# More up products ahead of the down products: 47 instead of 39, six of them behind the last one-hot product

## The chip, the cores and the metric

The kernel runs on one core of one Trainium2 chip. The metric is the time of one execution in device microseconds (us). The kernel before took 1903.67 us, the median of three runs (1903.01 to 1905.06).

Engines are named as the profile names them: PE is TensorE (PEld its weight loads), DVE VectorE, ACT ScalarE, POOL GpSimd, SP SyncE. SP issues the ordinary transfers of this kernel, in order, and POOL issues the indexed gathers.

## The reference, cut to what matters

The block is attention plus a gated recurrence (untouched here), and then PEER, a lookup of 128 single-neuron experts (8 heads, 16 each) out of 16384 for each of 512 tokens:

```python
def one_block(hb):                       # 128 tokens of h = RMSNorm(x)
    ...                                  # sc: scores of 8 heads x 2 x 128 keys
    top_s, pos = lax.top_k(cand_s, PEER_TOPK)
    idx = jnp.take_along_axis(cand_i, pos, axis=-1)      # i1 * 128 + i2
    g = jax.nn.softmax(top_s, axis=-1)
    u = u_tab[idx]
    act = jax.nn.gelu(jnp.einsum('thkd,td->thk', u, hb))
    wts = (g * act.astype(jnp.float32)).astype(hb.dtype)
    v = v_tab[idx]
    return jnp.einsum('thk,thkd->td', wts, v)
...
x = x + peer_ffn(rms_norm(x, norm2_g), w_peer_q, peer_sub_keys, peer_u, peer_v)
```

## The kernel before, in words

The 512 tokens are four blocks of 128. Two blocks gather the rows of `u` and `v` of their own experts (`experts()`): for each of 128 experts per token POOL issues one gather of 128 rows of 8 KB (tile `uv`, 1.05 MB), DVE multiplies the u half with the token and sums (L862), ACT makes the weight (L867, L868), and DVE adds the weighted v half to the result (L845). The second of these blocks (`second()`, tiles `h2g`, `x1g`) runs beside the part that follows; `share()` doles out its experts: 0.2 for each up product of `ups_far`, 0.5 for each one-hot group, 0.6 for each down product alone, and 1.1 for each down product with an up product beside it. A gather is placed behind the last gelu, copy or `o` product then written (`turn[0]`).

The other two blocks (256 tokens) are done densely over all 16384 experts, in 128 chunks of 128. Three kinds of products make this up:

- **Up products** (`up()`, 128): one chunk of `u` (512 KB) against the 256 tokens, then gelu into a tile `y`. The first 39 in the order of `TURN` are *ahead* (`c < AHEAD`): `u` as it is, in fp32, against `p1.h2r`, 8 matmuls which the trace shows as 16. The other 89 are *near*: `chunk()` splits `u` into a high and a low fp32r part (an ACT cast, L906, and a DVE subtraction, L907), and three products of parts are summed, 24 matmuls against `p1.h2T`, the operand that the keys used too.
- **One-hot products** (`wbuild()`, 16 groups of 16 tokens): DVE writes one-hot tiles `o2` (L994), DVE, POOL and ACT write weighted one-hot tiles `o1s`, PE multiplies them into `pw`, ACT copies to `wst`, and SP stores each group to DRAM (`w_d`, 1 MB). A load turns `w_d` into `w`, the weight of every expert of a chunk for all 256 tokens; it comes in tiles of 12 chunks (1.5 MB), the first in three pieces, the last of which (L1023, groups 14 and 15) needs the last group's store.
- **Down products** (`down()`, 128): DVE makes `o = y * w` (L1035), and PE adds `o` times the chunk of `v` into `acc`, 8 matmuls of 128x512. One load brings two chunks of `v` (1 MB, L1031).

The order in the program: 26 up products ahead (`LEAD`, `ups_far`, psum tile `pup`) stand beside the last picks of the keys on DVE (L258 to L334). `picks_t` turns the picks on PE (tile `pt`). Then come the 16 one-hot groups, with one up product (psum tile `st`) after each while fewer than `AHEAD - 6` are made, and a loop for the rest. Then come 128 down products; from down product 24 on (`HEAD`) each one has a near up product behind it, until all 128 are made. Results ahead wait in 24 slots of two `rg` tiles and 15 tiles of the pool `mid`. Everything carries an order from a scheduler at build time: an up product written behind the last one-hot group may be put ahead of it where its operands allow.

The pool `ap` (the keys' operand `p1.h2T`, two parts of 128x2048) is open to the end of the kernel. `trunk` holds pools of the earlier part, and its room is given to `mid` when it closes.

## Time and profile before

| | us |
|---|---|
| median of 3 runs | 1903.67 |
| the profiled execution | 1902.58 |
| its span in the profile | 1900.8 |
| PE busy | 1742.3 (92%) |
| DVE busy | 1309.5 (69%) |
| ACT busy | 781.8 (41%) |
| PE, down products (`acc`) | 449.9, 1024 matmuls |
| PE, near up products (`st<-a,t`) | 282.2, 2136 matmuls |
| PE, up products ahead (`pup`, `st<-r,u`) | 90.6 and 48.1, 416 and 208 matmuls |

Busy time is time in which an engine had an instruction of its own running. The chain that ended last goes from the last instruction backward, at each step to what released it; idle time of an engine counts only where the chain goes through what it waited for. The part that the change touches lies from 1015 us to the end: the last picks (to 1046), one-hot products beside up products (to 1116), one-hot products alone (to 1175), a junction (to 1194), 24 down products alone (to 1277), down and near up products in turn (to 1845), and 16 last down products. Matmul records can be missing by a few per cent.

### The profile page before, as it was taken

The numbers are of one execution on the slowest core, as the hardware profiler recorded it, in microseconds if no ns is written. First come the engines' busy times: TensorE is split into PE (matmuls) and PEld (weight loads), VectorE is DVE, ScalarE is ACT, GpSimd is POOL, SyncE is SP. The second block draws the span as 40 slices with busy tenths as digits, with TensorE's granted clock in tenths as the row PEclk, the third lists the DMA queues.
The fourth block names the chain that finished last, engine by engine and source line by source line (L and its number), as shares of the span: only waits on it lengthen the run. The fifth ranks groups of instructions, "written<-read, shape, count | busy, mean of one in ns | idle before, by whom it ended". The sixth has DMA issues, their size and how long they took to land.

```text
span 1900.8 us, 25745 instructions
## 1 busy us (share of the span) xinstructions
PE 1742.3 (92%) x9166; PEld 1371.8 (72%) x9166; DVE 1309.5 (69%) x2818; ACT 781.8 (41%) x2193; POOL 483.3 (25%) x375
## 2 busy tenths in 40 slices
PE   7899898889959899979996984899999999999998
PEld 6689797778849677769985884346776677667763
DVE  2241387989999987689999467446676667666662
ACT  3382333767768744254412565012322232222210
POOL 1100001535332233242001365222222232222220
PEclk9899897889969899999998998899999999999999
DMA  7478554887888899987464578999999999999893
GB/s 297 144 272 315 181 186 158 308 291 269 328 287 298 322 400 356 369 310 255 153 220 144 183 274 310 356 373 393 370 367 389 378 365 369 348 350 363 328 354 122
DMA packets 131471, 563.37 MB, mean 296 GB/s; under 512 B 11408, under 2 KB 43280, under 8 KB 88592
## 3 DMA queue, kind: packets, MB, share of 16 engines
q1 hardware_dynamic: 94480, 293.29, 42.6%
q0 software_dynamic: 36864, 268.45, 37.3%
q8 instruction: 72, 1.18, 0.2%
q14 instruction: 55, 0.45, 0.1%
HBM read 539.68 MB, written 22.02 MB: 296 GB/s over the span
## 4 chain that ended last, share of the span: by engine, by line
PE 60%; DVE 14%; issue 9%; DMA 8%; ACT 5%; POOL 3%; DVEq 0%; SPq 0%; POOLq 0%; ACTq 0%
PE acc L210 22%; PE st L210 16%; DMA uv<-in_uv_dram,idx 6%; PE ppq L210 5%; PE pkq L210 5%; POOL uv L855 3%; DVE x1f L845 2%; DVE uv L862 2%; PE pw L1010 1%; PE pvv L210 1%; DMA v<-in_v_t_dram 1%; PE pgt L210 1%; PE psc L511 1%; DVE wl L231 1%; PE pbR L687 1%
## 5 line engine op out<-in xcount | busy, mean ns | idle before, releaser
L855 POOL DMA_INDIRECT uv<-in_uv_dram,idx x256 | 360.0, 1406 | 1067.6 <-DVE x1g L845 265.7
L210 PE MATMUL acc<-v,o 128*128 128x512 f32 x1024 | 449.9, 595 | 20.8 <-DVE o L1035 18.6
L210 PEld LDWEIGHTS acc<-v,o 128*128 128x128 f32 x1024 | 191.8, 191 | 244.9 <-issue 222.4
L210 PE MATMUL st<-a,t 128*128 128x256 f32 x2136 | 282.2, 292 | 0.0
L210 PEld LDWEIGHTS st<-a,t 128*128 128x128 f32 x2136 | 262.5, 191 | 22.5 <-issue 19.6
L845 DVE SCALAR_TENSOR_TENSOR x1g<-uv,e,x1g 128x1024 f32<-128x1024 f32 x128 | 164.1, 1282 | 47.6 <-ACT e L868 47.6
L845 DVE SCALAR_TENSOR_TENSOR x1f<-uv,e,x1f 128x1024 f32<-128x1024 f32 x128 | 163.8, 1280 | 17.2 <-ACT e L877 17.0
L862 DVE SCALAR_TENSOR_TENSOR uv<-uv,h2f 128x1024 f32<-128x1024 f32 x128 | 155.6, 1218 | 28.9 <-DMA uv<-in_uv_dram,idx 28.5
L862 DVE SCALAR_TENSOR_TENSOR uv<-uv,h2g 128x1024 f32<-128x1024 f32 x128 | 155.9, 1218 | 19.6 <-DMA uv<-in_uv_dram,idx 19.6
L867 ACT ACTIVATE e<-e 128x1 f32<-128x1 f32 x128 | 25.9, 202 | 341.4 <-DVE uv L862 341.0
L907 DVE TENSOR_TENSOR t<-raw,t 128x1024 fp32r<-128x1024 f32 x89 | 108.8, 1223 | 74.5 <-ACT t L906 74.5
L1035 DVE TENSOR_TENSOR o<-y,w 128x256 f32<-128x256 f32 x104 | 44.0, 423 | 99.8 <-PE acc L210 99.7
L924 ACT ACTIVATE y<-st 128x256 f32<-128x256 f32 x89 | 34.1, 383 | 179.7 <-PE st L210 177.5
L231 DVE TENSOR_TENSOR wl<-raw,wh 128x1024 fp32r<-128x1024 f32 x76 | 90.9, 1217 | 23.8 <-PE pgt L210 9.5
L906 ACT CAST t<-raw 128x1024 fp32r<-128x1024 f32 x89 | 92.0, 1034 | 25.1 <-PE acc L210 25.1
L210 PE MATMUL pup<-r,u 128*128 128x256 f32 x416 | 90.6, 379 | 1.0 <-DMA u<-in_u_t_dram 1.0
L230 ACT CAST wh<-raw 128x1024 fp32r<-128x1024 f32 x76 | 76.7, 1043 | 28.2 <-PE pwo L714 10.4
L210 PEld LDWEIGHTS pup<-r,u 128*128 128x128 f32 x416 | 78.7, 190 | 12.3 <-issue 1.7
L1010 PE MATMUL pw<-o1s,o 128*128 128x128 f32 x512 | 68.8, 289 | 17.7 <-DVE o L994 13.3
L1009 POOL TENSOR_SCALAR o1s<-iota,r 128x128 f32<-128x128 bf16 x64 | 70.8, 1114 | 41.7 <-issue 14.8
L1010 PEld LDWEIGHTS pw<-o1s,o 128*128 128x128 f32 x512 | 64.5, 199 | 22.8 <-ACT wst L1011 5.7
L210 PE MATMUL pkq<-wh,a 128*128 128x256 f32 x384 | 77.8, 297 | 0.0
(266 smaller groups left out, 3235.5 us busy)
## 6 DMA issues: line engine op xcount, KB each, us to landing
v<-in_v_t_dram SPq DMA_DIRECT2D x64, 1024.0 KB
raw<-in_u_t_dram SPq DMA_DIRECT2D x89, 512.0 KB
u<-in_u_t_dram SPq DMA_DIRECT2D x39, 512.0 KB
w<-in_w_br_dram SPq DMA_DIRECT2D x16, 1024.0 KB
w_d<-wst SPq DMA_DIRECT2D x16, 1024.0 KB
w<-w_d SPq DMA_DIRECT2D x9, 1536.0 KB
w<-in_w_qkv_dram SPq DMA_DIRECT2D x12, 1024.0 KB
raw<-in_w_qkv_dram SPq DMA_DIRECT2D x24, 512.0 KB
```

The costliest lines, as they stand in the source:

```text
L210: nc.tensor.matmul(o, lhs[a], rhs[b], start=start and i == 0, stop=stop and i == len(terms) - 1)
L230: A.copy(hi[:, i : i + 1024], raw)
L231: V.tensor_tensor(lo[:, i : i + 1024], raw, hi[:, i : i + 1024].bitcast(F32), op=ALU.subtract)
L845: V.scalar_tensor_tensor(x1, v_, e_, x1, op0=ALU.mult, op1=ALU.add)
L855: i = nc.gpsimd.indirect_dma_start(out=t, out_offset=None, in_=uv, in_offset=bass.IndirectOffsetOnAxis(ap=idx[:, s : s + 1], axis=0),)
L862: i = V.scalar_tensor_tensor(t[:, 0:D], t[:, 0:D], 1.0, h2, op0=ALU.mult, op1=ALU.mult, accum_out=d)
L906: A.copy(t[:, 0, :], raw)
L907: V.tensor_tensor(t[:, 1, :], raw, t[:, 0, :].bitcast(F32), op=ALU.subtract)
L924: return A.activation(o, S_, AF.Gelu_apprx_tanh)
L1009: e.tensor_scalar(o1, iota, k1, g1, op0=ALU.is_equal, op1=ALU.mult)
L1010: nc.tensor.matmul(pw[:, j, :], o2[:, j, :], o1, start=True, stop=True)
L1035: turn[0] = V.tensor_mul(o.rearrange("p (g t) -> p g t", g=NG), yv, ws[c // WI][:, :, c % WI, :])
```

## The change

Eight more up products are ahead: 47. They come from eight results kept in a new tile `spare` (128 x 8 x 256).

- The pool `ap` becomes one of `trunk`'s, and the keys of the last three blocks are written ahead of `trunk.close()`. `mid` then lies where `p1.h2T` was as well. So the near up products take another operand: `h2s`, two tiles in `mid`, written by one ACT cast of `p1.h2r` and one DVE subtraction, both 128x2048 and both new instructions.
- `LEAD` goes from 26 to 31: five more up products stand in `ups_far`.
- The loop over the one-hot groups takes up products while fewer than `AHEAD - HELD` = 41 are made: 10 of them, where it was 7 (33).
- The last `HELD` = 6 are tied: the first matmul of each has an order dependence on the last one-hot product. It is one of the build order alone; at run time they are on the same engine. The 6 that were written behind the loop before had no tie.
- Near up products are 81 where they were 89, and the first is written behind down product 32 where it was 24. The shares of `second()` go with that.

```diff
-    HEAD, MID = 24, 15
-    AHEAD = HEAD + MID
+    HEAD, MID, SPARE = 24, 15, 8
+    AHEAD = HEAD + MID + SPARE
...
-    LEAD = 26
+    LEAD, HELD = 31, 6
...
-    def up(c, S_):
+    def up(c, S_, after=None):
         ks = lambda k: slice(k * P, (k + 1) * P)
         if c < AHEAD:
             u = wp.tile([P, D], F32, tag="raw", name=nm("u"), bufs=3)
             nc.sync.dma_start(u, u_t[c])
             for k in range(KT):
-                mm(S_, [u[:, ks(k)]], [p1.h2r[:, k, :]], k == 0, k == KT - 1)
+                i = mm(S_, [u[:, ks(k)]], [p1.h2r[:, k, :]], k == 0, k == KT - 1)
+                if after is not None and k == 0:
+                    tc.add_manual_dep(i.ins, after.ins.name, in_turn, reason="in turn")
         else:
             uhi, ulo = chunk(u_t, c, "near")
             for k in range(KT):
-                mm(S_, [uhi[:, ks(k)], ulo[:, ks(k)]], [h[:, k, P : 3 * P] for h in p1.h2T], k == 0, k == KT - 1)
+                mm(S_, [uhi[:, ks(k)], ulo[:, ks(k)]], [h[:, k, :] for h in h2s], k == 0, k == KT - 1)
...
         for tg in range(NG):
-            wbuild(tg)
+            last = wbuild(tg)
             share("w")
-            if len(ys) < AHEAD - 6:
+            if len(ys) < AHEAD - HELD:
                 up_near()
...
         wload(0, 14, NG)
         while len(ys) < AHEAD:
-            up_near()
+            up_near(last)
+
+        A.copy(h2s[0], p1.h2r)
+        V.tensor_tensor(h2s[1], p1.h2r, h2s[0].bitcast(F32), op=ALU.subtract)
         for c in range(NCH):
             down(c, ys[c])
-            if c >= HEAD and len(ys) < NCH:
+
+            more = c >= HEAD + SPARE and len(ys) < NCH
+            if more:
                 up_near()
-            share("both" if c >= HEAD and len(ys) < NCH else "down")
+            share("both" if more else "down")
```

The scheduler puts the two new instructions for `h2s` far ahead of where they are written: among the picks on DVE, near 936 us of the trace of before.

PE at the start of the one-hot stage, before (`pup` and `st` are up products, `pt3` turns the picks, `pw` are one-hot products):

```order
L210 MATMUL pup_1836_9261<-r_1193_6202,u_1837_9262 128x256 x8
L932 MATMUL pt3_1842_9286<-ident_92,r_1211_6281 128x128 x3
L932 MATMUL pt3_1843_9295<-ident_92,r_1211_6281 128x128 x3
L1010 MATMUL pw_1846_9318<-o1s_1844_9316,o2_1847_9319 128x128 x4
L1010 MATMUL pw_1849_9332<-o1s_1844_9316,o2_1850_9333 128x128 x4
L210 MATMUL st_1858_9375<-r_1193_6202,u_1859_9376 128x256 x7
L1010 MATMUL pw_1852_9346<-o1s_1844_9316,o2_1853_9347 128x128 x4
```

The same place after:

```order
L210 MATMUL pup_1848_9332<-r_1193_6202,u_1849_9333 128x256 x8
L938 MATMUL pt3_1854_9357<-ident_92,r_1211_6276 128x128 x3
L938 MATMUL pt3_1855_9366<-ident_92,r_1211_6276 128x128 x3
L210 MATMUL st_1870_9446<-r_1193_6202,u_1871_9447 128x256 x8
L210 MATMUL st_1888_9524<-r_1193_6202,u_1889_9525 128x256 x4
L1018 MATMUL pw_1858_9389<-o1s_1856_9387,o2_1859_9390 128x128 x4
L1018 MATMUL pw_1861_9403<-o1s_1856_9387,o2_1862_9404 128x128 x4
L210 MATMUL st_1888_9524<-r_1193_6202,u_1889_9525 128x256 x4
```

One and a half up products now stand between `pt3` and the first `pw`. Further on, before, 13 up products alternate with the one-hot products of the first 6 groups, and 10 groups follow alone; after, 10 up products alternate with the first 4 groups, and 12 groups follow alone.

PE at the junction, the end of the one-hot products and the first down products, before:

```order
L1010 MATMUL pw_2092_10368<-o1s_2084_10338,o2_2093_10369 128x128 x4
L1010 MATMUL pw_2095_10382<-o1s_2084_10338,o2_2096_10383 128x128 x4
L210 MATMUL acc_9315<-v_2113_10479,o_2114_10481 128x512 x4
L210 MATMUL acc_9315<-v_2113_10479,o_2115_10487 128x512 x4
L210 MATMUL acc_9315<-v_2118_10500,o_2119_10502 128x512 x4
```

And after:

```order
L1018 MATMUL pw_2110_10475<-o1s_2102_10445,o2_2111_10476 128x128 x4
L1018 MATMUL pw_2113_10489<-o1s_2102_10445,o2_2114_10490 128x128 x4
L210 MATMUL st_2118_10512<-r_1193_6202,u_2119_10513 128x256 x8
L210 MATMUL st_2120_10524<-r_1193_6202,u_2121_10525 128x256 x8
L210 MATMUL st_2122_10536<-r_1193_6202,u_2123_10537 128x256 x8
L210 MATMUL st_2124_10548<-r_1193_6202,u_2125_10549 128x256 x8
L210 MATMUL st_2126_10560<-r_1193_6202,u_2127_10561 128x256 x8
L210 MATMUL acc_9386<-v_2131_10588,o_2132_10590 128x512 x3
L210 MATMUL st_2128_10572<-r_1193_6202,u_2129_10573 128x256 x8
L210 MATMUL acc_9386<-v_2131_10588,o_2132_10590 128x512
```

Five of the six tied up products stand between the last one-hot product and the first down product, and the sixth inside the first down product.

SP at the same place, before (`w_d` are the last two groups' stores, `w` the loads of the weights, `v` those of the down products):

```order
L1012 DMA w_d_172<-wst_2071_10280 128x2048
L1031 DMA v_2113_10479<-in_v_t_dram 128x2x1024
L1031 DMA v_2118_10500<-in_v_t_dram 128x2x1024
L1031 DMA v_2123_10521<-in_v_t_dram 128x2x1024
L1012 DMA w_d_172<-wst_2085_10339 128x2048
L1023 DMA w_1979_9901<-w_d_172 128x2x192
L1023 DMA w_2112_10477<-w_d_172 128x16x192
```

And after:

```order
L1020 DMA w_d_172<-wst_2089_10387 128x2048
L1040 DMA v_2131_10588<-in_v_t_dram 128x2x1024
L1040 DMA v_2136_10609<-in_v_t_dram 128x2x1024
L1020 DMA w_d_172<-wst_2103_10446 128x2048
L1040 DMA v_2141_10630<-in_v_t_dram 128x2x1024
L919 DMA u_2125_10549<-in_u_t_dram 128x1024
L919 DMA u_2127_10561<-in_u_t_dram 128x1024
L1032 DMA w_1993_9984<-w_d_172 128x2x192
L919 DMA u_2129_10573<-in_u_t_dram 128x1024
L1032 DMA w_2130_10586<-w_d_172 128x16x192
```

The loads for the fourth to sixth tied up product now stand around the last piece of the first `w`, behind three loads of `v`. There are three buffers for `u`, so the fourth waits until the first tied up product has been computed.

## Rows read from the trace of the kernel before

**Rows 1.** The chain that ended last, 1040 to 1350 us: start, length, what
```profile
1042.79 1.23 DVE r L321
...
1110.53 1.80 PE pw L1010 x16
1112.35 0.70 DVE o L994
1113.21 8.70 DMA uv<-in_uv_dram,idx
...
1131.99 10.76 DMA uv<-in_uv_dram,idx
...
1176.36 14.34 DMA w_d<-wst
1190.72 2.65 DMA w<-w_d
1193.97 37.26 PE acc L210 x81
1231.23 22.39 DMA v<-in_v_t_dram
1253.76 24.27 PE acc L210 x56
...
1331.90 5.75 PE st L210 x48
1337.65 6.87 PE acc L210 x16
```

**Rows 2.** Timeline of PE: start, length, instructions, idle time before and its releaser
```profile
1015.65 10.60 PE L210 MATMUL pup<-r,u 128*128 128x256 f32 x48 [0.95 <-DMA u<-in_u_t_dram]
1037.93 0.88 PE L932 MATMUL pt<-ident,r 128*128 128x128 f32 x3 [11.68 <-DVE r L321]
1044.07 0.90 PE L932 MATMUL pt<-ident,r 128*128 128x128 f32 x3 [5.26 <-DVE r L321]
1046.43 3.78 PE L1010 MATMUL pw<-o1s,o 128*128 128x128 f32 x16 [1.46 <-ACT kTb L937]
...
1104.69 1.95 PE L1010 MATMUL pw<-o1s,o 128*128 128x128 f32 x16
1106.48 4.05 PE L210 MATMUL st<-r,u 128*128 128x256 f32 x18
1110.37 1.95 PE L1010 MATMUL pw<-o1s,o 128*128 128x128 f32 x16
...
1115.61 9.91 PE L1010 MATMUL pw<-o1s,o 128*128 128x128 f32 x72
...
1173.32 2.02 PE L1010 MATMUL pw<-o1s,o 128*128 128x128 f32 x16 [0.67 <-ACT wst L1011]
1193.97 6.56 PE L210 MATMUL acc<-v,o 128*128 128x512 f32 x9 [18.63 <-DVE o L1035]
```

**Rows 3.** Engines by stretch: us, busy time of each engine, granted clock, DMA share, GB/s
```profile
1115.00:1176.00 61.00, 44.06 (x324) 39.78 (x322) 52.93 (x123) 46.59 (x121) 47.34 (x40) 0.97 0.76 289
1180.00:1190.00 10.00, 0.00 (x0) 0.00 (x0) 1.23 (x2) 0.50 (x2) 0.00 (x0) 0.50 0.85 319
1196.00:1231.00 35.00, 35.00 (x80) 15.41 (x79) 15.70 (x24) 2.49 (x10) 8.63 (x6) 0.96 1.03 398
1231.00:1277.00 46.00, 43.84 (x103) 19.14 (x102) 22.98 (x36) 5.58 (x16) 10.84 (x8) 1.00 1.00 370
1277.00:1350.00 73.00, 73.00 (x379) 51.44 (x378) 48.21 (x62) 20.17 (x46) 18.54 (x14) 1.00 1.00 382
1838.00:1900.00 62.00, 56.23 (x139) 25.26 (x138) 18.71 (x30) 2.76 (x11) 3.46 (x3) 0.99 0.46 176
```

**Rows 4.** The page: a DMA queue (packets, MB, share), and a group of instructions
```profile
q0 software_dynamic: 36864, 268.45, 37.3%
...
L907 DVE TENSOR_TENSOR t<-raw,t 128x1024 fp32r<-128x1024 f32 x89 | 108.8, 1223 | 74.5 <-ACT t L906 74.5
```

## What the time will be, predicted before the run

> **What bounds the kernel now.** I read the chain of waits first, for the stretch from the last picks to the near up products [rows 1]. It shows five stages with different limits. Up to 1044 us the chain is on DVE: the last reduction of the picks, `r` L321, is what PE's `pt` waits for. From 1046 to 1112 it is PE, one-hot and up products in turn. From 1112 to 1175 it hops between DVE, PE and transfers, with two gathers of 8.70 and 10.76 us in it. Then a store of the last group (14.34) and the reload of it (2.65) stand alone in the chain, and from 1194 it is PE to the end, but for a wait for one `v`, which the chain shows as 22.39 us of transfer.
>
> PE's timeline gives the size of its waits in these stages [rows 2]. The last `pup` ends at 1026.25 (1015.65 + 10.60), then PE is idle 11.68, 5.26 and 1.46 us before the first `pw` at 1046.43. The second hole is at the junction: the last `pw` ends at 1175.34, and the first down product starts at 1193.97, after 18.63 us that the reader should see as the largest single hole of the whole dense part. The windows show how PE stands elsewhere [rows 3]: in the one-hot products alone PE is busy 44.06 of 61 us and DVE 52.93, so DVE and what it waits for are the limit there; from 1196 on PE is full, except 2.16 us in 1231 to 1277 (46.00 less 43.84), and the DMA share is 1.00 to 1.03 at the same time. So the down products run close to two limits at once, which matters below.
>
> **Prices.** A near up product and a down product: the chain shows 48 `st` matmuls in 5.75 us, that is 2.875 for one of 24, and 16 `acc` in 6.87, that is 3.435 for one of 8 [rows 1]. An up product ahead: from 1106.48 to 1110.37 are 3.89 us for 18 rows of the trace, so 3.46 for 16. A one-hot product is 1.78 us for 16 rows (1104.69 to 1106.48), and a group has 32 [rows 2]. So an up product ahead costs 0.59 us more than a near one, and the change can only win by putting it where PE waits now.
>
> **Part 1, the lead: five more `pup`.** 48 rows took 10.60 us [rows 2], or 3.5 for one product; five need 17.5 and fill the hole that begins at 1026.25, to 1043.7. The picks end at 1044.0 (1042.79 + 1.23) [rows 1]. The copy and subtraction for `h2s` are new on ACT and DVE among the picks; the subtraction is twice the width of L907, which takes 1.22 us [rows 4], so 2.4 us on the engine that ends this stage. Against it, some one-hot work that DVE did ahead of the last reduction now stands behind it (about 2 us). One and a half up products stand ahead of the first `pw`, so ACT's copy of the picks no longer shows on PE. I put the start of the stage at 1045, with 0 to 4 us later as the bound if none of the 2.4 is given back.
>
> **Part 2, the one-hot stage.** 10 up products (34.6) and the one-hot products of 4 groups (128 rows at 0.111, 14.2) are PE's: 48.8 us, to 1094. Then 12 groups stand alone. Before, 10 groups alone took from 1115.61 to 1175.34, 5.97 each [rows 2]; 12 take 71.6, to 1165.6. That is 9.7 us earlier than before. Bounds: by DVE's busy time alone (52.93 of 61 us, 5.2 a group) [rows 3] the stage ends at 1156.5 and the gain is 19; with a start 4 us later it is 5.7. I take 9.7, since the waits for gathers come with the share of 0.5 per group, which stays.
>
> **Part 3, the junction.** Before: 18.63 idle, and the first 9 `acc` took 6.56 instead of 9 x 0.43 = 3.86 at a granted clock that had fallen to 0.50 in the idle stretch [rows 2, 3]: 1.2 GHz, half of the 2.4 that the 1.00 rows stand for. So 21.3 us from the last `pw` (call it T) lead nowhere. After: six up products, 6 x 3.46 = 20.8 us, do work there, and the clock has no reason to fall. The store and reload chain is about as long (14.34 + 2.65, then `o`), and hides under them. But the loads for the fourth to sixth stand behind three `v` loads and around the last piece of `w` in SP's order, the fourth waits for the first product, and the sixth for that piece. At some 382 GB/s [rows 3], what is queued by then (three `v` of 1.05 MB, the store of 1.05, one gather of 1.05, `u` of 0.52 each) is 6.8 MB, or 18 us from about T - 4; the sixth `u`, issued at about T + 15.5, lands near T + 19. With the products behind it that is T + 21.5 at best, T + 28 if each load is late; I take T + 25. Against 21.3 that is **+3.7** (0 to +7).
>
> **Part 4, the down products.** Eight near up products fewer, each 2.875 us in a stretch where PE is full at clock 1.00 [rows 1, 3]: **-23.0**. Their ACT casts and DVE subtractions go too, which were hidden. What hides nothing any more is the transfer: 32 down products instead of 24 now run without an up product. One down product alone asks for half a `v` load (0.524 MB), 0.6 of a gather (268.45 MB in 256 gathers [rows 4], 1.05 each: 0.63) and a twelfth of a `w` (0.131): 1.285 MB in 3.435 us, or 374 GB/s. The trace moved 398, then 370 there [rows 3]. Counting from T to the 31st down product: the last store 1.05, 17 `v` loads 17.8, six `w` and a piece 9.6, 19 gathers 19.9, three `u` 1.6, together 49.9 MB. At 382 GB/s, about the mean of these two rows, that is 131 us; PE gets there in 25 + 30 x 3.435 = 128. At 398 it is 125, no wait; at 370, 135, a wait of 7. Unevenness comes on top, as in the 2.16 of before. I take **+5** (0 to +10). The last 16 down products keep room for what `second()` still owes, 5.5 experts instead of 2.5 by the sums of the shares: DMA share 0.46, DVE 18.71 of 62 us [rows 3].
>
> **Sum.** -9.7 + 3.7 - 23.0 + 5 = -24.0. Of the profiled execution of 1902.58 us that leaves 1878.6; the median of the runs is 1.1 above that execution, so **1879**.
>
> **A rule against it.** With PE full the queues moved 398 GB/s over 35 us and 382 over 73 [rows 3]. The Trainium skill, "DMA: Bandwidth & Descriptors", section "Where 436 GB/s comes from", says that for transfers between HBM and SBUF the HBM side binds, at about 358 GB/s for one core; the trace does not agree. By 358 the 49.9 MB would take 139 us, a wait of 11, and each down product with a near one (2.33 MB) 6.52 us instead of 6.31, so 17 more over 81: about 1902. Nothing of the sum uses this figure.
>
> **The rivals.** (A) *The one-hot stage does not end earlier.* If the work of DVE and POOL, not PE's place, sets when the last group is done, T stays at 1175 and part 2 is lost: 1889. For it: DVE is the limit for the last 60 us. Against: DVE is held back by PE in the first 66 us, since the chain there is PE alone [rows 1], and two groups fewer have to wait for that.
>
> (B) *No transfer is late.* The tied products end at T + 21 and the queue moves 398: -32.7 and 1870. For it: the up products give the queue 21 us of PE time in which the first `v` and `w` land.
>
> (C) *The junction becomes a wait for loads, and the kernel slower.* One `v` load issued at 1231.23 took 22.39 us to land behind what was queued [rows 1]. If the last store and the piece of `w` take that each, where 14.34 and 2.65 are seen now, the first `o` comes at T + 47; three `acc`, the sixth up product and a restart at the lower clock (2.7, as above) bring the down products to T + 55 instead of T + 25: +30, 1909. It loses from T + 46 on. Against: the store took 14.34 with the same three `v` loads ahead of it; now two stand ahead of it, and the third behind.
>
> (D) *The up products fill no idle time.* If PE waits for the same things as long as before, eight products at 3.46 replace eight at 2.875: +4.7, 1908. It needs both holes of [rows 2] to remain, and the instructions between them now say otherwise.
>
> (E) *The queue is the limit from T to the end*, as its share of 1.00 beside a full PE suggests [rows 3]. At the 370 GB/s of the second row, a down product with a near one (0.52 of `v`, 0.52 of `u`, 1.1 gathers, 0.13 of `w`: 2.33 MB) takes 6.31, no loss; a rate lower by 3% costs 16 us there and 6 more in part 4: about 1901. The share of the rows says that there is little to spare, the full PE that there is some.
>
> **How the numbers follow.** Chances: the forecast (1872 to 1885) 0.58, A 0.13, B 0.11, C 0.07, D 0.03, E 0.08. The range, 1864 to 1893, holds the forecast, A, most of B and the bounds of parts 2 to 4, and leaves out C, D and E. A measurement of this kernel can tell a change of about 0.2%, 3.8 us, from none. Faster by more: forecast, A, B and a little of E, 0.83; within it: most of E and the mild ends of C and D, 0.07; slower: the rest of C, D and E, 0.10.
>
> **What would show it.** Right, if PE's timeline has `pup` to about 1044 and no idle row over 2 us ahead of the first `pw`; the last `pw` near 1166 (part 2; at 1175 it is A); `st` rows in the 20 us behind it, with a granted clock near 1.00 and the first `acc` of full speed at T + 25 (at T + 46 or later it is C); waits of PE for `v` or `o` in the first 32 down products of about 5 us in sum; and 1944 rows of near up products (81 x 24) at 2.875 us per product. Wrong, if the near up products' stage shows idle PE time at DMA share 1.00 (E), or if the copy for `h2s` holds the picks up, with the last reduction of the picks later than 1048.

## The result, and the profile after

The changed kernel took 1884.4 us (median of 4 runs, 1875.7 to 1886.7) beside 1903.3 for the kernel before: 0.989 of its time, 95% interval 0.987 to 0.991. The forecast was 1879. The profiled execution took 1883.81 (span 1882.0, where it was 1900.8), so the parts below are those of 18.8 us.

PE's timeline of the changed kernel, the stretch from the last `pup` to the down products (start, length, what, count, idle time before and its releaser):

```profile
1009.82 28.22 PE L210 MATMUL pup<-r,u 128*128 128x256 f32 x130
1039.67 0.52 PE L938 MATMUL pt<-ident,r 128*128 128x128 f32 x3 [1.64 <-DVE r L324]
1042.91 0.87 PE L938 MATMUL pt<-ident,r 128*128 128x128 f32 x3 [2.71 <-DVE r L324]
1043.58 6.70 PE L210 MATMUL st<-r,u 128*128 128x256 f32 x24
...
1093.76 9.82 PE L1018 MATMUL pw<-o1s,o 128*128 128x128 f32 x72
...
1158.90 4.54 PE L1018 MATMUL pw<-o1s,o 128*128 128x128 f32 x24 [2.08 <-DVE o L1002]
1163.28 10.53 PE L210 MATMUL st<-r,u 128*128 128x256 f32 x48
1180.63 9.92 PE L210 MATMUL st<-r,u 128*128 128x256 f32 x32 [6.82 <-DMA u<-in_u_t_dram]
1190.39 2.74 PE L210 MATMUL acc<-v,o 128*128 128x512 f32 x6
1192.96 3.62 PE L210 MATMUL st<-r,u 128*128 128x256 f32 x16
...
1252.88 43.95 PE L210 MATMUL acc<-v,o 128*128 128x512 f32 x96 [3.94 <-DMA v<-in_v_t_dram]
1300.16 9.86 PE L210 MATMUL acc<-v,o 128*128 128x512 f32 x16 [3.33 <-DMA v<-in_v_t_dram]
1309.46 2.45 PE L210 MATMUL st<-h2s,t 128*128 128x256 f32 x16
```

Against [rows 2] the reader sees both holes gone: PE idles 1.64 and 2.71 us at the end of the picks where it idled 11.68 and 5.26, and the 18.63 us ahead of the first `acc` hold `st` rows. In their place stand three new waits, all for loads: 6.82 for the `u` of the fourth tied product, and 3.94 and 3.33 for `v`. The matmuls behind each are slow for a while: 32 `st` rows took 9.92 us where 32 take 6.92, and 16 `acc` rows 9.86 where 16 take 6.87.

The chain of waits of the changed kernel, from the last one-hot product on, names the same three (start, length, what):

```profile
1166.93 13.56 DMA u<-in_u_t_dram
1180.63 9.92 PE st L210 x32
1190.55 2.58 PE acc L210 x6
1193.12 3.45 PE st L210 x16
1196.58 33.26 PE acc L210 x78
1229.83 22.91 DMA v<-in_v_t_dram
1252.88 24.82 PE acc L210 x52
1277.70 22.33 DMA v<-in_v_t_dram
1300.16 9.86 PE acc L210 x16
...
1341.93 5.66 PE st L210 x48
```

In both waits for `v` DVE wrote its last `o` early, up to 1249.39 and 1297.29 us, and the next one only when PE ran again; the `v` landed at 1252.74 and 1300.03 (start plus length of its two rows). So PE waited for the load and not for DVE.

The windows of the changed kernel around them (us, busy time of PE, PEld, DVE, ACT and POOL, granted clock, DMA share, GB/s) show a lower granted clock behind each wait (2.4 GHz is 1.00, the level below is 1.2), the DMA share near 1 up to it, and a lower one soon after:

```profile
1180.00:1190.00 10.00, 9.37 (x31) 7.82 (x32) 1.09 (x3) 0.38 (x1) 0.94 (x1) 0.69 1.05 371
1190.00:1200.00 10.00, 10.00 (x34) 6.19 (x33) 2.94 (x4) 1.26 (x4) 0.94 (x1) 1.00 0.61 220
...
1210.00:1220.00 10.00, 10.00 (x24) 4.37 (x23) 5.72 (x9) 0.79 (x4) 2.72 (x3) 1.00 1.02 412
...
1250.00:1260.00 10.00, 7.12 (x11) 3.14 (x12) 1.50 (x3) 0.00 (x0) 1.61 (x2) 0.66 0.96 389
1260.00:1270.00 10.00, 10.00 (x24) 4.37 (x23) 5.72 (x10) 0.99 (x4) 3.20 (x2) 1.00 0.71 241
...
1300.00:1310.00 10.00, 9.84 (x18) 4.37 (x19) 1.97 (x4) 0.50 (x2) 0.94 (x1) 0.71 0.68 274
```

The sum of the 18.8 us, with T for the end of the last `pw` (1175.3 before, 1163.4 after):

| | before | after | difference |
|---|---|---|---|
| T | 1175.3 | 1163.4 | -11.9 |
| from T to the down products at full pace | 21.3 | 30.4 | +9.1 |
| near up products (89 x 2.875, 81 x 2.825) | 255.9 | 228.8 | -27.1 |
| waits and slow matmuls behind them, from there to the last `acc` | 2.0 | 13.1 | +11.1 |

The second row of "after" is 1196.41 less the six `acc` done already (2.6), from T. The price of a near product comes from rows of 48 in 5.65 us (the one shown has 5.66), where [rows 1] has 5.75. The last row is what is left of the time to the last `acc` (1875.45; 1894.25 before) when the products, a down product at 3.435, are taken off; 12.8 of the 13.1 stand in the rows above (3.94 + 3.33, and 2.5 + 3.0 of slow matmuls).

### The profile page after: what moved, and what is told of

The parts are those of the page before. It is cut to its first block, busy times and chain, and to the rows that moved or that the text cites. A ratio compares the mean times of both kernels' runs of the same rounds, so it can differ in the third digit from the quotient of the medians.

```text
span 1882.0 us, 25603 instructions
## 1 busy us (share of the span) xinstructions
PE 1737.3 (92%) x9102; PEld 1361.6 (72%) x9102; DVE 1304.0 (69%) x2811; ACT 779.1 (41%) x2188; POOL 497.5 (26%) x375
## 4 chain that ended last, share of the span: by engine, by line
PE 63%; DVE 14%; DMA 11%; ACT 6%; issue 5%; POOL 1%; DVEq 0%; SPq 0%; POOLq 0%; ACTq 0%
PE acc L210 22%; PE st L210 15%; DMA uv<-in_uv_dram,idx 6%; PE ppq L210 5%; PE pkq L210 4%; PE pgt L210 3%; DMA v<-in_v_t_dram 2%; PE pbR L690 2%; DVE x1f L848 2%; PE pvv L210 2%; DVE uv L865 2%; PE pw L1018 2%; PE pbA L683 1%; PE psc L514 1%; PE prx L210 1%
## 5 line engine op out<-in xcount | busy, mean ns | idle before, releaser
L858 POOL DMA_INDIRECT uv<-in_uv_dram,idx x256 | 367.3, 1435 | 1077.9 <-DVE x1g L848 267.3
L210 PE MATMUL acc<-v,o 128*128 128x512 f32 x1024 | 452.3, 598 | 7.3 <-DMA v<-in_v_t_dram 7.3
L210 PEld LDWEIGHTS acc<-v,o 128*128 128x128 f32 x1024 | 193.3, 192 | 235.1 <-issue 230.2
L210 PE MATMUL st<-h2s,t 128*128 128x256 f32 x1944 | 252.6, 288 | 0.0
L210 PEld LDWEIGHTS st<-h2s,t 128*128 128x128 f32 x1944 | 235.0, 188 | 20.1 <-issue 17.2
L865 DVE SCALAR_TENSOR_TENSOR uv<-uv,h2g 128x1024 f32<-128x1024 f32 x128 | 156.1, 1219 | 31.1 <-DMA uv<-in_uv_dram,idx 31.1
L865 DVE SCALAR_TENSOR_TENSOR uv<-uv,h2f 128x1024 f32<-128x1024 f32 x128 | 155.6, 1218 | 28.7 <-DMA uv<-in_uv_dram,idx 27.8
L911 DVE TENSOR_TENSOR t<-raw,t 128x1024 fp32r<-128x1024 f32 x81 | 99.0, 1223 | 69.5 <-ACT t L910 69.5
L210 PE MATMUL pup<-r,u 128*128 128x256 f32 x496 | 107.6, 379 | 0.0
L210 PEld LDWEIGHTS pup<-r,u 128*128 128x128 f32 x496 | 94.0, 190 | 13.1 <-issue 0.4
L910 ACT CAST t<-raw 128x1024 fp32r<-128x1024 f32 x81 | 83.8, 1034 | 25.2 <-PE acc L210 25.0
L1017 POOL TENSOR_SCALAR o1s<-iota,r 128x128 f32<-128x128 bf16 x64 | 76.3, 1201 | 19.1 <-PE pw L1018 7.9
L201 POOL TENSOR_SCALAR sm<-sm 128x1 f32<-128x1 f32 (+4 forms) x24 | 10.9, 453 | 253.3 <-ACT hh L403 110.3
```

Source lines behind the costliest of these rows:

```text
L210: nc.tensor.matmul(o, lhs[a], rhs[b], start=start and i == 0, stop=stop and i == len(terms) - 1)
L858: i = nc.gpsimd.indirect_dma_start(out=t, out_offset=None, in_=uv, in_offset=bass.IndirectOffsetOnAxis(ap=idx[:, s : s + 1], axis=0),)
L865: i = V.scalar_tensor_tensor(t[:, 0:D], t[:, 0:D], 1.0, h2, op0=ALU.mult, op1=ALU.mult, accum_out=d)
L910: A.copy(t[:, 0, :], raw)
L911: V.tensor_tensor(t[:, 1, :], raw, t[:, 0, :].bitcast(F32), op=ALU.subtract)
L1017: e.tensor_scalar(o1, iota, k1, g1, op0=ALU.is_equal, op1=ALU.mult)
```

## The experiments

Each kernel is the changed kernel with one edit, but for e1 (none) and for e7, e8, e11 and e12, which have more. Two theories stood against each other. **Transfers:** what was lost behind T is queue time; the down products and the gathers beside them ask for about what the queues move, and every piece that stands ahead of a `v` or `u` in SP's order becomes a wait of PE. **PE or order:** the loss belongs to the order of PE's own work (the tie, the lead, where the near products start), whatever the loads do. The table has the median, T, what lay from T to the down products at full pace, and from T to the last down product in the profiled execution.

| | median us | T | T to full pace | T to the last `acc` |
|---|---|---|---|---|
| before | 1903.3 | 1175.3 | 21.3 | 719.0 |
| changed | 1884.4 | 1163.4 | 30.4 | 712.0 |
| e1 changed, again | 1884.2 | 1165.2 | 30.2 | 710.5 |
| e2 near from 24 | 2212.8 | 1165.8 | 30.4 | 1038.9 |
| e3 `v` behind `u` | 1880.0 | 1167.8 | 20.9 | 706.6 |
| e4 untied | 1887.6 | 1175.3 | 23.3 | 704.4 |
| e5 `w` spread | 1881.1 | 1159.9 | 28.1 | 711.2 |
| e6 fewer gathers | 1889.0 | 1168.0 | 28.3 | 706.5 |
| e7 both orders | 1873.0 | 1169.2 | 22.0 | 697.6 |
| e8 operand only | 1901.1 | 1173.9 | 21.1 | 714.6 |
| e9 lead of 26 | 1890.1 | 1180.3 | 28.3 | 702.5 |
| e10 no gathers | 1872.3 | 1168.2 | 28.4 | 697.1 |
| e11 start at 24, ring of 23 | 1874.1 | 1164.7 | 28.4 | 698.9 |
| e12 e11 and both orders | 1885.0 | 1167.4 | 22.3 | 709.0 |

T itself moves: ten of these runs have the lead of 31 and the tie, and their T lies between 1159.9 and 1169.2 (mean 1166.0). A difference of T of some us between two of them says nothing about their edits. The runs of one kernel spread by up to 12.5 us (1884.5 to 1897.0 in e4; those of the changed kernel in its two sets, 1875.7 to 1886.7), and the kernel before, run beside each of the four sets, had medians from 1901.8 to 1904.1. So 3 to 5 us between the medians of two kernels are hardly clear of noise.

### e1: the changed kernel again

> The changed kernel as it is, beside the others on the same chip, so that they can be compared with it and not only with the kernel before. If its profile is typical: last one-hot product near 1163 us, one wait for a tied up product's load near 7 us, two waits for v of 3 to 4 us each among the first 32 down products, and a time near 1884. One of its four runs took 1875.7; if the waits for v are a matter of chance from run to run, the times spread again over some 10 us.

1884.18, ratio 0.990 (0.987 to 0.993). One wait for a `u` (8.05 us), then one for `v` (3.18) and, in the place of the second one for `v`, one of 3.56 up to 1300.41 that the trace puts down to DVE's work on a gathered row (L865). It is most likely the same `v` again: the `o` was written at 1297.3, and the `v` load issued at 1278.19 took 22.1 us, to 1300.3. So the places hold.

### e2: the near products from down product 24

```diff
-            more = c >= HEAD + SPARE and len(ys) < NCH
+            more = c >= HEAD and len(ys) < NCH
```

> One number is undone: the near up products start behind down product 24 again, not 32; all 47 ahead stay. Theory (rate): the down products alone ask for about as many bytes as the queues move, and the second wait for v, near 1297 us, comes because the stretch is 8 products longer. Then that wait (3.3 us) and the slow matmuls behind it (3 us) go, the first one stays: 1878. Rival (backlog): the waits come from what piled up at the junction, whatever follows; both stay and the time is 1884, within 2 us. A second rival, that the gathers of the stage with both products now start earlier and wait more: 1886 or above, with waits for v between 1280 and 1350 us.

2212.8 us: 328 slower than the changed kernel, and no theory had that. PE waited 248.4 us for `v`, 32 times. Two timelines of this kernel over one turn of it, PE and then SP, and a row of ACT:

```profile
1508.61 8.63 PE L210 MATMUL acc<-v,o 128*128 128x512 f32 x16 [7.63 <-DMA v<-in_v_t_dram]
1516.67 6.21 PE L210 MATMUL st<-h2s,t 128*128 128x256 f32 x48
1530.86 9.44 PE L210 MATMUL acc<-v,o 128*128 128x512 f32 x16 [7.98 <-DMA v<-in_v_t_dram]
```

```profile
1519.61 3.27 SPq L908 DMA_DIRECT2D raw<-in_u_t_dram  x2
1522.97 0.39 SPq L1040 DMA_DIRECT2D v<-in_v_t_dram  x1
1542.68 3.06 SPq L908 DMA_DIRECT2D raw<-in_u_t_dram  x2
1545.83 0.40 SPq L1040 DMA_DIRECT2D v<-in_v_t_dram  x1
```

```profile
1514.30 0.38 ACT L930 ACTIVATE y<-st 128x256 f32<-128x256 f32 x1 [10.89 <-DVE o L1044]
```

The results of near products go into the 15 slots of `mid`; the eight in `spare` are not used again. Started at 24, the near products run out of slots when the down products reach 39, since these then free only `spare`. From there a gelu waits 10.89 us for the `o` that frees its slot, the cast of the next `u` stands behind it on ACT (and waits 2.59 us more there for PE's `acc`), so the load buffer stays full, SP holds the next `raw` load, and the `v` load behind that goes out only when it is needed. It is a lock step, one turn in 22 us for two down products. So the start at 32 in the change is no choice of pace: it follows from where the results lie. e11 tests the start without that.

### e3: `v` behind the tied products' `u`

The second and third `v` load, the last piece of the first `w` and the second `w` are ordered behind the `u` load of the fifth tied product:

```diff
-            nc.sync.dma_start(u, u_t[c])
+            loads.append(nc.sync.dma_start(u, u_t[c]))
...
+                i = nc.sync.dma_start(vs[-1], v_t[c : c + 2].rearrange("c p d -> p c d"))
+                if 2 <= c < 6:
+                    tc.add_manual_dep(i.ins, loads[-2].ins.name, in_turn, reason="in turn")
```

> The second and third load of v, and the last piece of the first w and the second w, are ordered behind the load of u for the fifth tied up product; PE's order is that of the changed kernel. Theory (queue): the fourth u took 13.6 us from issue to landing because two v loads, the store and a gather were ahead of it in the queues; now it lands within 6 us of its issue, PE's 6.8 us of waiting and the 3 us of slow matmuls behind it go, and the down products start 21 to 23 us behind the last one-hot product instead of 30.5. Of these 8 to 9 us some come back as later waits for v, since the same bytes are still to be moved: net 3 to 8 us faster than the changed kernel. Rival (buffer): the u is late because it waits for the first tied product's buffer; then it lands as late as before and the time is unchanged.

1879.96, ratio 0.987 (0.985 to 0.990): 4 us below the changed kernel, within the spread of runs but where transfers put it (3 to 8). PE's timeline of e3:

```profile
1167.67 17.77 PE L210 MATMUL st<-r,u 128*128 128x256 f32 x80
...
1223.47 30.24 PE L210 MATMUL acc<-v,o 128*128 128x512 f32 x64 [7.11 <-DMA v<-in_v_t_dram]
1256.18 42.98 PE L210 MATMUL acc<-v,o 128*128 128x512 f32 x96 [2.47 <-DMA v<-in_v_t_dram]
```

Five tied products run without a wait, and the down products start 20.9 us behind T instead of 30.4. So the fourth `u` was late for what stood ahead of it in the queue, not for its buffer. And the gain is asked back 30 us later: a wait of 7.11 for `v` that the changed kernel did not have. Of 9.5 us some 5 are left from T to the last `acc`.

### e4: untied

```diff
-            up_near(last)
+            up_near()
```

> The tie is taken away: all else of the change stays, and the scheduler puts the last six up products ahead among the one-hot products. Theory: the hole at the junction comes back (18 to 19 us idle with a clock of 0.5 in it), and the one-hot stage ends later by six up products less what they hide there: 16 up products and 7.4 groups to 1126, then 8.6 groups at 5.8 us, last one-hot product near 1176; down products from 1198 instead of 1194: 4 us slower than the changed kernel, or equal if the v loads that land in the hole save the waits for v later. Rival (the tie is what pays): 10 us or more slower than the changed kernel.

1887.6, ratio 0.992 (0.990 to 0.995): 3 us slower than the changed kernel, where the theory had 4, and little more than the noise. T is 1175.3 and the hole is back, as PE's timeline of e4 has it:

```profile
1196.16 57.52 PE L210 MATMUL acc<-v,o 128*128 128x512 f32 x128 [20.90 <-DVE o L1044]
```

So the tie moves 21 us of PE's work into the hole and is worth some 3 us of time. In these two executions T comes 11.9 us earlier by it; the rest of the 21 had filled waits of PE in the one-hot stage (from 1046 to 1163 us PE is busy 106.4 us in e4 and 98.5 in the changed kernel). Of the 11.9, 7.1 are given back at the junction (30.4 against 23.3), most of it to the wait for the fourth `u`. The `v` waits are no part of the difference: e4 has 6.4 us of them in two pieces, the changed kernel 7.3.

### e5: the loads of `w` spread

Two pairs of `w` loads (3.1 MB each) stood in SP's order just ahead of the two late `v` loads. Here each later `w` is ordered behind the `v` load of the down product at which the program asks for it:

```diff
             if c % WI == 0 and len(ws) * WI < NCH:
                 wtile()
-                wload(len(ws) - 1)
+                wload(len(ws) - 1, after=i if c else None)
```

(`i` is the `v` load, written ahead of it, and `wload` adds the dependence.)

> Of the changed kernel, the loads of the third and later w tiles are ordered behind the v load of the down product that is 12 ahead of their first use; so they no longer stand in pairs (3.1 MB) ahead of one v load. Theory (burst): both waits for v in the changed kernel follow such a pair (pairs at 1225 and 1273 us, the v behind them took 22 to 23 us to land); spread, each v lands within 15 us, the waits (7.3 us) and the slow matmuls behind them (5.7) go, and the time is 1871 to 1875. Rival (rate): the queues are full in this stretch whatever the order; then waits of 5 us or more stay and the time is 1880 or above.

1881.1, ratio 0.988 (0.985 to 0.992). The first 32 down products run through, without one wait, and the waits come in the stage behind, for `v` and for the casts of near products. PE's timeline of e5, and then what PE waits for from 1310 to 1800 (us, times, longest):

```profile
1190.59 104.02 PE L210 MATMUL acc<-v,o 128*128 128x512 f32 x242
...
1325.29 3.70 PE L210 MATMUL acc<-v,o 128*128 128x512 f32 x8 [1.50 <-DMA v<-in_v_t_dram]
```

```profile
PE acc L210 <- DMA v<-in_v_t_dram: 3.5, 2, 2.0
PE st L210 <- DVE t L911: 3.3, 2, 2.6
PE st L210 <- ACT t L910: 1.5, 1, 1.5
```

From T to the last `acc` it is 711.2, as before the edit. So the burst theory held for the place (its two waits went) and not for the price (1871 to 1875 was expected). What came in their place is in part loads again: two casts waited 5.2 us on ACT for `raw`, the `u` of a near product, where in the changed kernel that was 0.3. That it is the same bytes, moved, is not shown.

### e6: fewer gathers beside the first down products

```diff
-    SHARE = {"far": 0.2, "w": 0.5, "down": 0.6, "both": 1.1}
+    SHARE = {"far": 0.2, "w": 0.5, "down": 0.45, "both": 1.1}
```

> Of the changed kernel, the share of experts for a down product alone is 0.45 instead of 0.6: 5 gathers (5 MB) fewer in the first 32 down products, and as many more at the end. Theory (burst): 13 us of queue time are taken out, but the pairs of w loads still stand ahead of a v load each; at least one of the two waits stays, at 1 to 4 us, and the time is 1878 to 1882. Rival (rate): demand falls from 374 to 328 GB/s and both waits go: 1871 to 1875. If the end of the kernel cannot hide the 5 experts, each costs some 2.5 us of DVE there, at most 12 us, and the last down product is not what ends last.

1889.0, ratio 0.992 (0.990 to 0.995): 5 us slower than the changed kernel. The first 32 down products again run without a wait, though the pairs of `w` loads stand where they stood (1228.75 and 1269.15 us). So "at least one of the two waits stays" was wrong: either less demand or a better order is enough, and the pair alone is no cause. One wait for `v`, of 3.35 us, came later, at 1338. The time was lost at the end: by the sums of the shares about 10 experts were left for the last 16 down products, and the chain leaves PE at 1857 us for DVE and a gather of 7.11 us, with the last `x1g` ending the kernel. The last `acc` ended at 1874.5, 1 us before that of the changed kernel; the span ended 14.2 us behind it, where it was 6.6.

### e7: both orders of loads

e3 and e5 in one.

> Both orders of loads in one: v behind the tied products' u, and the w loads spread. Theory (burst, and bytes put off at the junction): the first order alone started the down products some 5 us sooner and paid it back in one wait of 7 us for v, at a pair of w loads; with the pairs gone the gain stays: 4 to 8 us below the kernel with the spread w loads alone, 1865 to 1870. Rival (rate): what is gained at the junction is waited for later: within 2 us of the kernel with spread loads alone.

1873.0, ratio 0.983 (0.979 to 0.986): 11 us below the changed kernel, and with e11 (1874.1, no clear difference) the fastest complete kernel of this study. The wait for the fourth `u` is 1.25 us, and the matmuls behind it are not slow; 234 rows of `acc` run through. PE's timeline, and then a window of 100 us:

```profile
1180.79 7.14 PE L210 MATMUL st<-r,u 128*128 128x256 f32 x32 [1.25 <-DMA u<-in_u_t_dram]
...
1193.80 100.59 PE L210 MATMUL acc<-v,o 128*128 128x512 f32 x234
```

```profile
1200.00:1300.00 100.00, 100.00 (x237) 44.51 (x237) 55.31 (x83) 10.44 (x36) 24.98 (x17) 1.00 1.00 385
```

It fell short of 1865 to 1870 in part by its T, 1169.2, which is 3 us above the mean of the ten, and in part by 4.5 us in four pieces in which PE waited for the casts and subtractions of near products.

### e8: the operand alone

The kernel before with the near products' new operand and the new places of pools and keys; 39 ahead, a lead of 26, no tie:

```diff
-    HEAD, MID, SPARE = 24, 15, 8
+    HEAD, MID, SPARE = 24, 15, 0
...
-    LEAD, HELD = 31, 6
+    LEAD, HELD = 26, 6
...
-            up_near(last)
+            up_near()
```

> The kernel before with one part of the change alone: the near up products take their operand from the two new tiles, 39 ahead, no spare results, 26 in the lead, no tie. Theory: the operand is why a near product took 2.83 instead of 2.875 us in the changed kernel; 89 of them give 4 us, so 1899 to 1900, with 283 us or less for... the near products' matmuls' mean falls from 292 to 288 ns. Rival: the mean stays at 292 (the price fell for another reason), and the time is that of the kernel before, within 2 us. The two instructions that write the tiles cost at most 2.4 us among the picks.

1901.05 (10 runs), ratio 0.9997 (0.998 to 1.001): the time shows no gain. The profile does: the near products' matmuls, as the page has them for e8 and [rows 1] and the table of the profile before have them for before (2136 rows, 282.2 us), are

```profile
L210 PE MATMUL st<-h2s,t 128*128 128x256 f32 x2136 | 278.9, 288 | 0.1
```

and 48 of them take 5.65 us in the chain, where they took 5.75. From T to the last `acc` is 4.4 us less. So the price of a near product fell with its operand, by 0.05 us each; that the 4.4 us of 89 of them reach the time, this measurement doesn't show. What about the operand does it (a tile of 256 columns instead of 256 out of 384, or its new place) was not tried.

### e9: a lead of 26

```diff
-    LEAD, HELD = 31, 6
+    LEAD, HELD = 26, 6
```

> Of the changed kernel, the lead goes back to 26 up products; the five stand beside the one-hot groups instead, 15 there. Theory: PE idles 11 and 5 us before the one-hot stage again, as in the kernel before, and the last one-hot product comes near 1176 instead of 1163 to 1168: about 10 us slower, 1893 to 1895, unless waits for transfers behind it shrink by some of that. Rival (the one-hot stage is set by DVE, POOL and gathers alone): the last one-hot product comes as early as with 31 in the lead, and the time is 1884 within 3 us.

1890.1, ratio 0.993 (0.990 to 0.995): 6 us slower than the changed kernel, where 9 to 11 were expected. PE's timeline of e9 has the hole again, and T is 1180.3, some 14 us later than with 31:

```profile
1045.20 0.88 PE L938 MATMUL pt<-ident,r 128*128 128x128 f32 x3 [18.49 <-DVE r L324]
1050.28 0.90 PE L938 MATMUL pt<-ident,r 128*128 128x128 f32 x3 [4.20 <-DVE r L324]
```

Two cautions: the picks ended 7 us later in this kernel (the second `pt` at 1050.28, in e8 with the same lead at 1043.35), for a reason I did not find, so about half of those 14 us are the hole; and some 8 of the 14 come back behind T (702.5 us instead of 710.5 and 712.0).

### e10: no gathers beside the down products

The second gathering block stops after its first 14 experts; 114 of its 128 are left out, with their gathers and their work on DVE.

```diff
-        for s in range(SLOTS):
+        for s in range(14 if table else SLOTS):
```

> Of the changed kernel, the second gathering block ends after its first 14 experts, which are done by the junction; its other 114 experts are left out, so that no gather and none of their DVE work runs beside the down products. PE's own work from the last one-hot product to the last down product is 6 x 3.46 + 128 x 3.435 + 81 x 2.83 = 690 us; the changed kernel took 712. Theory (transfers): nearly all of those 22 us are waits for loads and the slow matmuls behind them; without gathers none of the waits for v stays, the wait for the fourth tied product's load may stay in part (5 us): 1862 to 1868. Rival (PE or the order): 10 us or more of the loss stay with PE waiting for something else or its matmuls longer, 1872 or above.

1872.3, ratio 0.984 (0.981 to 0.987). What PE waits for in this kernel, from T on, is one row; the other rows of the answer lie ahead of T. Then two windows:

```profile
PE st L210 <- DMA u<-in_u_t_dram: 6.2, 1, 6.2
```

```profile
1200.00:1300.00 100.00, 100.00 (x234) 44.27 (x233) 13.69 (x31) 1.19 (x2) 0.00 (x0) 1.00 0.67 226
1300.00:1400.00 100.00, 100.00 (x493) 67.63 (x492) 25.89 (x33) 20.18 (x29) 0.00 (x0) 1.00 0.58 195
```

The 697.1 us from T to the last `acc` are the 689.3 of PE's own work and the 7.6 by which the down products started late (28.4 less 20.8). Nothing else is left: the 13.1 us of the changed kernel behind its junction go with the gathers. The time was 4 to 10 us over what was expected, on the rival's side of 1872, and T was 1168.2 here, not 1163.4, which is 5 of them; the argument rests on the row of waits, not on the time. PE's order and its own work are not the cause of these 13 us. This run takes DVE's work for the gathers away together with their transfers, so it doesn't tell the two apart; that the two waits of the changed kernel were for loads is in its own rows above.

### e11: the near products from 24, with a ring of 23 slots

```diff
-        if HEAD + MID <= c < AHEAD:
-            return spare[:, c - HEAD - MID, :]
         if c >= HEAD:
-            return mid.tile([P, NT2], F32, tag="ym", name=nm("y"), bufs=MID)
+            return mid.tile([P, NT2], F32, tag="ym", name=nm("y"), bufs=MID + SPARE)
...
-            more = c >= HEAD + SPARE and len(ys) < NCH
+            more = c >= HEAD and len(ys) < NCH
```

> The near up products start behind down product 24, as in e2, but the eight spare results are slots of the same ring as the other 15 (23 slots), so a near result can be put into each slot that a down product frees. Theory (e2's loss of 330 us was a lock step: gelu waits for a slot, the casts queue behind it on ACT, so the load buffer stays full and the v load behind it on SP waits): gone; near products are done with 24 down products left instead of 16, and about 5 gathers more are left to that end. The stretch of down products alone is 24 long, so the second wait for v goes: 1876 to 1882. Rival (rate): the same bytes wait in the stage with both products: 1884 within 3 us.

1874.1, ratio 0.985 (0.982 to 0.989): 10 us below the changed kernel. The lock step of e2 is gone with the ring, which shows that the slots were its cause. Between the junction (a wait of 5.94 us for the fourth `u`) and the last `acc` PE waits once, 1.65 us at 1249.8, where the changed kernel waited 7.3 in two pieces. The chain ends in `1781.15 82.41 PE acc L210 x192`: 24 down products alone at the end, which hide the experts that are left, where 16 could not hide as many in e6.

### e12: e11 with both orders of loads

> e11 with both orders of loads of e7. Theory: waits in the down stretch are gone by the orders already, so what e11 adds is what the end hides, 5 gathers of 2.7 us of queue time: 3 to 8 us below e7, 1865 to 1870. Rival: the 24 last down products cannot hide the 10 experts that are then left (e6: 10 experts did not fit 16 down products), and it is as e7 or slower, 1873 to 1880.

1885.0, ratio 0.990 (0.987 to 0.994): 12 us slower than e7 and 11 slower than e11, against both expectations. The down products start well (22.3 us behind T), the first stretch has no wait, and then PE waits 5.9 us in four pieces and 5.6 in five for the casts and subtractions of near products' `u` (e11: none there). Two of the casts waited 6.7 us on ACT for `raw`, and in e11 none did; what makes those loads late, and the other casts, was not separated, and stays open.

## Why the prediction was right, and where it was not

Direction, place and range were right: 1884 in 1864 to 1893, faster. The forecast of -24.0 met -18.8 in the profiled execution and -19 to -20 in the medians. (Its 1878.6 + 1.1 is 1879.7; 1879 is a slip.) That the miss is only 5 us is in part luck. The junction cost 5.4 us more than the forecast had and the waits of part 4 cost 6.1 more; part 2 gave 2.2 more and the near products 4.1 more, the latter for a reason that no step foresaw.

- **Part 1, the lead**: right. `pup` fills the hole (two waits of 1.64 and 2.71 us are left; "no idle row over 2 us" missed by 0.7). The subtraction for `h2s` took 2.28 us and holds nothing up: the last reduction ends at 1042.8, where it was 1044.0 [rows 1].
- **Part 2, T at 1165.6**: right. T was 1163.4 in the profiled execution and 1166.0 in the mean of ten. The 12 groups alone took 69.5 us, 5.79 each instead of 5.97. Rival A (T stays at 1175) is what e4 shows without the tie, and e9, with the caution on its picks, without the longer lead; so T does follow PE's place.
- **Part 3, the junction, +3.7**: the step that was mis-sized. It named the row that would be late (the fourth `u`, behind `v` loads and the store) and gave T + 25, "T + 28 if each load is late"; T + 30.4 was measured, +9.1. Two things are in the difference: the fourth `u` took 13.56 us from its issue at T + 3.5, in which the queues moved some 5 MB (404 and 371 GB/s in the windows from 1170 to 1190), and "the clock has no reason to fall" was wrong: behind a wait of 6.82 us it stood at 0.69, and 32 rows took 3.0 us more. Rival C had the kind of event, a load late at the junction and a restart at the lower clock, but for the store and the piece of `w` and at +30; and by its own sum it loses from T + 49 on, not from T + 46.
- **Part 4, near products, -23.0**: the count was right (1944 rows), the price not: -27.1, since the operand made each 0.05 us cheaper. No step asked what the new operand would do to a matmul.
- **Part 4, waits, +5 (0 to +10)**: +11.1, just above the upper bound. The bytes were counted well: by the 31st down product, where near products begin (1309.46, T + 146), the queues had moved some 52 MB, and 49.9 were counted. The rate was not: the fourteen windows of 10 us from 1170 to 1310 have a mean of 356 GB/s, where 382 was taken, since three of them stand at a DMA share of 0.61, 0.71 and 0.68: the stretches with PE's sixth tied product and those behind the two waits for `v`. Across the first of these waits POOL issued no gather between 1249.67 and 1259.79 (held by an `o`) and SP no `v` load between 1248.97 and 1262.52; across the second no gather came between 1297.15 and 1308.52 (held by `x1g`). So the queue that PE waited for ran thin soon after the wait. Missing as well were the slow matmuls behind the waits (5.5 of the 13.1 us).

**Rival E** and the rule against the change: the window of 100 us of e7 moved 385 GB/s, and one of 10 us of the changed kernel 412, with PE busy all the time in both. The Trainium skill's figure of about 358 GB/s ("DMA: Bandwidth & Descriptors", section "Where 436 GB/s comes from") does not bind this core alone; the trace decides. But the rival's first half, that the queue is what is short behind T, held: e10 takes the gathers away and the waits for `v` go, and e3 and e5 move a wait and pay it elsewhere.

What became of the rest of the gain is a matter of rate and not of bytes. From T to the last `acc` the kernel before, the changed one, e7, e9 and e11 all move 250 to 252 MB; in the first 146 us behind T the changed kernel moves 354 GB/s, the one before 374, and the other three 379 each. (e5 moves 353 there without a wait, and waits later.) PE's work was moved into holes as planned, ahead of T and at T. Only the hole at T had been much used by transfers (a DMA share of 0.82 and 297 GB/s from 1176 to 1196 us before; in the lead's hole, from 1020 to 1046, 0.32 and 102). What PE gains by being early it meets again as waits, in part, until the order of the loads (e7) or the length of the tail (e11) is changed as well. Why e9 needs 9.5 us less behind its T (702.5 against 712.0), with its T 17 us later, is not shown.

## What to carry to other kernels

When work is moved into a hole of the busiest engine, look up what the queues were doing in that hole: if they were nearly full, as at the junction here, the hole was time for transfers, and a part of the gain can come back as waits some loads later. Count a wait of PE at its length and the slow matmuls behind it, and look for it at the first load that stands behind a burst in the issuing queue. And where results lie in a ring, the slots set how early their producer may start: eight results in places that aren't used again cost 328 us when the producer started eight steps earlier, and nothing (10 us gained) when they joined the ring.

## What the runs showed of the hardware that was not expected

- The clock after a short wait. In the windows of the changed kernel the granted clock was 0.69, 0.66 and 0.71 (of 2.4 GHz; the level below is 1.2) in the 10 us from 1180, 1250 and 1300, behind waits of 6.82, 3.94 and 3.33 us, and the matmuls there lost 3.0, 2.5 and 3.0 us. The loss doesn't go by the length of the wait alone: 8.05 us in e1 cost 1.6 and 6.18 in e10 1.7; 2.47 in e3 cost 1.8, but 2.16 before [rows 3] and 2.62 in e9 only 0.2, as did 1.25 in e7.
- One 512 KB load took 13.56 us to land, and a 1 MB load 22.9, where the medians for these over the whole kernel are 3.7 and 8.5; both stood behind other loads in SP's order, the `u` behind three `v` loads and a store, the `v` behind a pair of `w` loads. In e3, with two of the three `v` loads ordered behind it, the `u` was in time.
- Near products' matmuls of 128x256 with an operand out of a tile of 256 columns took 288 ns in the mean, with one out of 384 columns 292 (e8 and before); 5.65 us instead of 5.75 for 48 in a row.
